# A chained gated MLP: one block split sooner, a sum's transfer put in front, the second gate before the first value

## The chip, the cores and the metric

The program runs on one core of a Trainium2 chip. A core has a matmul engine (PE in the profile, with its weight loads as PEld), a vector engine (DVE), an activation engine (ACT), a general engine (POOL) and a queue engine for loads (SP). Each runs its own list of instructions in order and waits on semaphores of the others. POOL issues the transfers that add while they copy; SP issues the plain loads. The metric is device time of one execution in microseconds.

## The reference

A trunk of two layers over 512 tokens of width 1024. Each layer has a token mixer, a cross attention into 256 memory tokens, and a gated MLP with a causal convolution of width 3 on its gate branch. The change lies in the MLP, and in the order of two loads for the attention's queries.

```python
def conv_ffn(x, norm, w_up, dw_w, dw_b, w_down):
    h = rms_norm(x, norm) @ w_up              # 1024 -> 2 * 3072
    g = causal_dwconv(h[..., :D_FF], dw_w, dw_b)
    u = h[..., D_FF:]
    return (jax.nn.gelu(g) * u) @ w_down      # 3072 -> 1024

for layer in range(DEPTH):                    # DEPTH = 2
    x = x + mixer(...)
    x = x + cross_attn(...)
    x = x + conv_ffn(...)
return rms_norm(x, final_norm)
```

## The kernel before

Data lies transposed, channels on the 128 partitions and the 512 tokens along the row. Every product is made of three matmuls of float32 operands that are split into a high part (ACT copies it, line 812) and a low part (DVE subtracts, line 819): high by high, high by low, low by high (lines 186 to 188).

The hidden width of 3072 is 24 chunks of 128. In each MLP the chunks 0 and 1 are computed plainly in `opening`; the chunks 2 to 23 are computed one by one in `unit(c)`, gate and value together, by a scheme with seven products instead of eight on blocks of half size. Its weight operands, by the names in the code, are `a11`, `a12`, `a22` (stored blocks) and `s1`, `s2`, `s3`, `s4` (sums of blocks). The sums are made in place by POOL's adding transfers (`low`, lines 817 to 830). A chunk's tile `raw` has two halves, `r` (first `a11`) and `z`:

- after the split of `a11`: `r += z` (line 822), and `r` is `s3`;
- after the split of `s3`: `r += a22` (line 826), and `r` is `s2`;
- after the split of `a22`: `z += a22` (line 824), and `z` is `s1`;
- after the split of `s2`: `r += a12` (line 830), and `r` is `s4`.

For the queries (tiles with a `ring`) both additions of `a22` stand at `s3` (lines 826 and 828).

Each of the seven products is twelve matmuls of 256 columns, called a piece here. PE's order in `unit(c)` is: `s1`, `s2`, `a12`, `s3`, then from unit 4 on 24 matmuls of the down projection, then `a11` of the next chunk (in `ahead`), `s4`, `a22`. `s2` adds onto a bank that ACT has filled from `a11`'s result (line 924), `s3` adds onto a bank that ACT has read first (line 941), and `s4` adds onto a bank that DVE has read first (line 171).

While PE works through unit c, ACT and DVE do two things between each other's steps, in the order of the code. They split blocks: in unit c the `s3`, `a22`, `a12`, `s1` and `s2` of chunk c+1, the `a11` of chunk c+2 and the `s4` of chunk c. And they finish the activation of chunk c-1 (`gating`: line 901 scale, 891 and 894 convolution, 896 GELU, 910 and 915). The order on PE, ACT, DVE and POOL is the order of the code in this part (`manual_schedule`); SP's order comes from the scheduler.

In `opening`, `start(i)` is the product of one plain weight piece, `gate(c)` is the scale, convolution and GELU of a plain chunk (lines 1012, 891, 894, 896, 1015), `values(c)` multiplies the value in and copies the high part (1018, 1020), `close(c)` makes the low part (1023). The token norm's mean is two matmuls (lines 287 and 288), followed by a root on ACT (1037) and a reciprocal on DVE (1040).

"First", "second" and "third unit" are chunks 2, 3 and 4. Units 2 and 3 have no down projection in them.

Of the kernel before, what the change touches and what calls it, by code (L numbers as in the profile page):

```python
# [61 lines left out]
def trunk(ctx: ExitStack, tc: tile.TileContext, I: dict, out: list):  # L62
    nc = tc.nc
    V, A, G, PE = nc.vector, nc.scalar, nc.gpsimd, nc.tensor
# [6 lines left out]
    tmp = ctx.enter_context(tc.tile_pool(name="tmp", bufs=8))  # L71
# [7 lines left out]
    def nm(s):  # L79
        uid[0] += 1  # L80
        return f"{s}_{uid[0]}"
# [16 lines left out]
    def main_ps():  # L98
        return psum.tile([P, T], F32, tag="mm", name=nm("mm"))
# [79 lines left out]
    def low(src, hi, lo=None):  # L179
        lo = act_r() if lo is None else lo  # L180
        V.tensor_tensor(lo, src, hi.bitcast(F32), op=ALU.subtract)  # L181
        return hi, lo
# [596 lines left out]
    class Blocks:  # L779
# [8 lines left out]
            self.r, self.z = raw[:, :T], raw[:, T:]  # L788

        def load_second(self):  # L790
            self.a22, self.a12 = [tmp.tile([P, T + 4], F32, tag="h", name=nm("wa"), bufs=4)[:, :T] for _ in range(2)]
            nc.sync.dma_start(self.a22, self.src[:, D : D + T])
            nc.sync.dma_start(self.a12, self.src[:, D + T :])

        def high(self, name):
            if self.ring:
# [20 lines left out]
        def low(self, name):  # L817
            hi, lo = self.w[name]
            V.tensor_tensor(lo, self.block(name), hi.bitcast(F32), op=ALU.subtract)  # L819

            if name == "a11":
                G.dma_start(self.r, self.z, accum_op=ALU.add)  # L822
            elif name == "a22" and not self.ring:
                G.dma_start(self.z, self.a22, accum_op=ALU.add)
            elif name == "s3":
                G.dma_start(self.r, self.a22, accum_op=ALU.add)  # L826
                if self.ring:
                    G.dma_start(self.z, self.a22, accum_op=ALU.add)
            elif name == "s2":
                G.dma_start(self.r, self.a12, accum_op=ALU.add)  # L830

# [3 lines left out]
    def ffn(layer, norm, nxt, seven, pairs):  # L835
# [37 lines left out]
        def high(c, name):  # L873
            if c in pairs and (c, name) not in done:
                pairs[c].high(name)

        def low(c, name):
            if c in pairs and (c, name) not in done:
                pairs[c].low(name)
                done.add((c, name))  # L880

        def times_r(out, ps, at):
            V.tensor_tensor(out[:, at], ps, norm.r[:, at], op=ALU.mult)
# [36 lines left out]
        def ahead(c):  # L920

            G, F = main_ps()[:, :M], main_ps()[:, :M]
            m(c, G, "a11", seven.B11)
            A.activation(F, G, AF.Copy)
            return G, F

        def unit(c):

            nonlocal left, chains
            G, F = chains  # L930
            down, seeded = downs.get(c), c > GC
            H = main_ps()[:, :M]
            m(c, H, "s1", seven.T1)
            high(c + 1, "s3")
            next(left, None)
            low(c + 1, "s3")

            m(c, F, "s2", seven.T2, False)
            next(left, None)
            u, f, g = tmp_f(), tmp_f(), tmp_f()  # L940
            A.activation(u[:, :M], F, AF.Copy)
            next(left, None)
            high(c + 1, "a22")

            m(c, G, "a12", seven.B21, False)
            next(left, None)
            if down:
                d = [down.bank(i, seeded) for i in range(2)]
            next(left, None)
            low(c + 1, "a22")  # L950
            times_r(g, G, left_half)
            high(c, "s4")

            m(c, F, "s3", seven.T3, False)
            A.activation(u[:, M:], F, AF.Copy)
            low(c, "s4")
            add(f[:, right_half], H, u[:, M:])
            V.tensor_tensor(f[:, right_half], f[:, right_half], norm.r[:, right_half], op=ALU.mult)
            high(c + 2, "a11")
            low(c + 2, "a11")  # L960
            high(c + 1, "a12")
            low(c + 1, "a12")
            if down:
                for ks in (range(GC - 1), (GC - 1,)):
                    for i in range(2):
                        down.products(i, d[i], seeded, ks)
            if c + 3 in pairs:
                pairs[c + 3].load()
            if c + 2 in pairs and c > first:
                pairs[c + 2].load_second()  # L970
            if c >= GC - 1 and c + 1 in downs:
                downs[c + 1].w.high()
                downs[c + 1].w.low()
            if c + 2 in downs and c + 2 <= CF:
                downs[c + 2].load()
            high(c + 1, "s1")
            low(c + 1, "s1")
# [12 lines left out]
            left = gating(c, g, f, u, F, H)  # L990
            next(left)

        def opening():
# [23 lines left out]
            def values(c):  # L1017
                V.tensor_tensor(y[c], ps.pop(2 * c + 1), y[c], op=ALU.mult)
                ys[c] = act_r(), act_r()
                A.activation(ys[c][0], y[c], AF.Copy)  # L1020

            def close(c):
                V.tensor_tensor(ys[c][1], y[c], ys[c][0].bitcast(F32), op=ALU.subtract)

            def both(c, name):
                high(c, name)
                low(c, name)

            ss = split(norm.ss)
            start(0)  # L1030
            fetch(2)
            w[-1].low()
            start(1, range(1))
            mean = mean_of(ss)
            Norm.due = None
            root = tmp_f()
# [1 line left out]
            A.activation(small.tile([P, 1], F32, tag="warm", name=nm("gelu"), bufs=1), eps, AF.Gelu_apprx_tanh)  # L1038
            norm.r = small.tile([P, T], F32, tag="r", name=nm("r"), bufs=1)
            V.reciprocal(norm.r, root)  # L1040
            start(1, range(1, C))
            pairs[second].load()
            pairs[second].load_second()
            fetch(3)
# [6 lines left out]
            t = seven.sums(3, lambda: (next(g), next(g)))  # L1051
# [2 lines left out]

            start(2)
            both(second, "a11")
            values(0)
            next(t, None)
            close(0)

            start(3)
            g = gate(1)
            next(g)
            both(second, "a22")
            next(g)
            next(g)
            next(g, None)
            chains = ahead(first)

            def rest():  # L1070
# [7 lines left out]
        first, second = PLAIN, PLAIN + 1  # L1078
# [807 lines left out]
```

## Time and profile before

| | |
|---|---|
| median of 3 runs | 1448.69 us (1446.52 to 1449.44) |
| profiled execution | 1447.83 us, of it 1446.0 us span |
| PE busy | 1424.8 us (99%) |
| DVE, ACT, POOL busy | 1079.0, 906.1, 318.2 us |
| mean granted PE clock | 0.997 |
| first MLP: opening to unit 4 | about 340 to 423 us from the span's start |
| second MLP: the same | about 1035 to 1119 us |

PE is busy nearly everywhere, so a change can only show where PE waits or runs at a lower clock. The two MLPs run the same code 695.41 us apart (first matmul of `ahead(first)`: 379.73 and 1075.14 us).

In a row of the timeline the columns are the start in us, the duration, engine, line, operation, output and inputs, count, and in brackets the engine's idle time before it with what ended it. Matmul durations overlap: a matmul of 256 columns is shown with 0.28 us, and the next starts 0.12 us after it. In a row of a stretch the columns are the stretch, its length, the busy time and count of each engine, the granted PE clock, the share of the DMA engines and GB/s.

### The profile page before, as it was taken

What the parts mean: (1) busy time and instruction counts of PE and PEld (TensorE: products, weight loads), DVE (VectorE), ACT (ScalarE), POOL (GpSimd) and SP (SyncE); (2) the same over time, 40 slices, a digit from 0 to 9 for tenths busy, and PEclk for the clock granted to TensorE, in tenths of its full rate; (3) what the DMA queues carried; (4) which work ended last, traced back from release to release, by engine and by line L of the source; (5) the groups of instructions that cost most, each with busy time, mean ns of one, the idle gap of its engine ahead of it and who ended that gap; (6) DMA issues with size and microseconds to landing.
All of it is one profiled execution on the core that took longest, in us unless ns stands there. A gap on an engine that the chain in (4) does not pass through costs nothing.

```text
span 1446.0 us, 22842 instructions
## 1 busy us (share of the span) xinstructions
PE 1424.8 (99%) x8650; PEld 1264.9 (87%) x8650; DVE 1079.0 (75%) x1796; ACT 906.1 (63%) x1592; POOL 318.2 (22%) x333
## 2 busy tenths in 40 slices
PE   9999999999999999999999999999998999999998
PEld 7888888988889999999988777898888999999997
DVE  6987776779776676676789997877787776676665
ACT  7678755667556666666655547667654665666664
POOL 0011310100122222222008992011002222222211
PEclk9999999999999999999999999999999999999999
DMA  8623232544487677677432364345437777777651
GB/s 294 199 77 99 88 131 68 119 112 140 103 188 177 161 175 175 156 181 166 131 126 88 117 176 144 96 96 131 114 99 178 171 181 163 164 181 165 162 130 59
DMA packets 80318, 205.36 MB, mean 142 GB/s; under 512 B 9040, under 2 KB 9552, under 8 KB 80208
## 3 DMA queue, kind: packets, MB, share of 16 engines
q1 hardware_dynamic: 51120, 151.20, 33.6%
q0 software_dynamic: 28800, 52.44, 20.7%
q8 instruction: 67, 1.10, 0.3%
q14 instruction: 43, 0.35, 0.1%
q10 hardware_dynamic: 288, 0.27, 0.1%
HBM read 146.21 MB, written 2.10 MB: 103 GB/s over the span
## 4 chain that ended last, share of the span: by engine, by line
PE 80%; issue 7%; DMA 5%; DVE 4%; ACT 2%; POOL 2%; SPq 0%; POOLq 0%; ACTq 0%; DVEq 0%
PE mm L188 19%; PE mm L187 19%; PE mm L186 19%; PE aux L186 7%; PE aux L187 7%; PE aux L188 7%; DMA raw<-wa 1%; PE mm L458 1%; DMA raw<-raw 1%; DMA raw<-in_wv 1%; DVE wlo L167 1%; POOL actf L1487 1%; ACT whi L166 1%; POOL act L167 0%; DMA wa<-in_wpair 0%
## 5 line engine op out<-in xcount | busy, mean ns | idle before, releaser
L186 PE MATMUL mm<-act,whi 128*128 128x512 f32 (+2 forms) x1061 | 369.4, 349 | 1.1 <-ACT whi L801 1.1
L187 PE MATMUL mm<-act,whi 128*128 128x512 f32 (+2 forms) x1061 | 369.4, 348 | 0.7 <-DVE act L181 0.4
L188 PE MATMUL mm<-act,wlo 128*128 128x512 f32 (+2 forms) x1061 | 369.1, 348 | 0.0
L186 PEld LDWEIGHTS mm<-act,whi 128*128 128x128 f32 x1061 | 200.6, 189 | 29.1 <-ACT whi L801 1.5
L187 PEld LDWEIGHTS mm<-act,whi 128*128 128x128 f32 x1061 | 200.8, 189 | 28.3 <-DVE act L167 1.0
L188 PEld LDWEIGHTS mm<-act,wlo 128*128 128x128 f32 x1061 | 200.8, 189 | 24.9 <-DVE wlo L167 0.6
L186 PE MATMUL mm<-bigr,bigr 128*128 128x256 f32 x704 | 201.3, 286 | 6.2 <-ACT bigr L812 4.0
L188 PE MATMUL mm<-bigr,bigr 128*128 128x256 f32 x704 | 200.8, 285 | 0.4 <-DVE bigr L819 0.4
L187 PE MATMUL mm<-bigr,bigr 128*128 128x256 f32 x704 | 200.5, 285 | 0.0
L812 ACT ACTIVATE bigr<-raw 128x512 fp32r<-128x512 f32 x176 | 105.2, 621 | 81.1 <-DMA raw<-wa 76.2
L186 PE MATMUL aux<-act,whi 128*128 128x512 f32 x399 | 155.8, 391 | 0.0
L187 PE MATMUL aux<-act,whi 128*128 128x512 f32 x399 | 155.7, 390 | 0.0
L188 PE MATMUL aux<-act,wlo 128*128 128x512 f32 x399 | 155.2, 389 | 0.0
L166 ACT ACTIVATE whi<-raw 128x1024 fp32r<-128x1024 f32 (+1 forms) x95 | 96.5, 1020 | 87.1 <-PE mm L187 46.4
L819 DVE TENSOR_TENSOR bigr<-raw,bigr 128x512 fp32r<-128x512 f32 x176 | 117.7, 688 | 41.9 <-ACT bigr L812 41.9
L186 PEld LDWEIGHTS mm<-bigr,bigr 128*128 128x128 f32 x704 | 136.4, 194 | 7.5 <-ACT bigr L812 4.4
L188 PEld LDWEIGHTS mm<-bigr,bigr 128*128 128x128 f32 x704 | 136.5, 194 | 0.9 <-DVE bigr L819 0.9
L187 PEld LDWEIGHTS mm<-bigr,bigr 128*128 128x128 f32 x704 | 136.5, 194 | 0.0
L822 POOL DMA_DIRECT2D raw<-raw x50 | 43.3, 866 | 361.4 <-DVE wlo L819 223.9
L171 DVE TENSOR_TENSOR tmp<-mm,tmp 128x256 f32<-128x256 f32 x130 | 53.9, 419 | 86.3 <-PE mm L188 84.6
L167 DVE TENSOR_TENSOR wlo<-raw,whi 128x1024 fp32r<-128x1024 f32 (+1 forms) x75 | 90.3, 1210 | 22.0 <-ACT whi L166 21.7
L826 POOL DMA_DIRECT2D raw<-wa x50 | 43.2, 863 | 282.2 <-DVE bigr L819 229.4
(355 smaller groups left out, 3122.4 us busy)
## 6 DMA issues: line engine op xcount, KB each, us to landing
raw<-wa POOLq DMA_DIRECT2D x150, 256.0 KB, 5.2
wa<-in_wpair SPq DMA_DIRECT2D x88, 256.0 KB, 3.4
raw<-in_wpair SPq DMA_DIRECT2D x44, 512.0 KB, 4.8
big<-in_wdown SPq DMA_DIRECT2D x44, 512.0 KB, 4.0
raw<-raw POOLq DMA_DIRECT2D x50, 256.0 KB, 4.5
raw<-in_pw SPq DMA_DIRECT2D x24, 512.0 KB, 3.3
raw<-in_win SPq DMA_DIRECT2D x20, 512.0 KB, 3.3
raw<-in_wk SPq DMA_DIRECT2D x16, 512.0 KB, 3.6
```

What stands on the lines that cost most here:

```text
L166: A.activation(hi, src, AF.Copy)
L167: fetched[1] = (eng or V).tensor_tensor(lo, src, hi.bitcast(F32), op=ALU.subtract)
L171: V.tensor_tensor(out, a, b, op=ALU.add)
L186: PE.matmul(ps, wh, xh, start=first, stop=False, skip_group_check=onto)
L187: PE.matmul(ps, wh, xl, start=False, stop=False, skip_group_check=onto)
L188: PE.matmul(ps, wl, xh, start=False, stop=last, skip_group_check=onto)
L458: PE.matmul(p, m[j], x, start=k == 0 and j == 0 and x is hi, stop=k == C - 1 and x is lo)
L812: A.activation(self.w[name][0], self.block(name), AF.Copy)
L819: V.tensor_tensor(lo, self.block(name), hi.bitcast(F32), op=ALU.subtract)
L822: G.dma_start(self.r, self.z, accum_op=ALU.add)
L826: G.dma_start(self.r, self.a22, accum_op=ALU.add)
L1487: G.tensor_tensor(z[:, s:], z[:, s:], f[:, s:], op=ALU.add)
```

## The change

Five edits, all in the order of instructions; no arithmetic is added or taken away.

1. In `unit`, in the first unit alone: the split of `a11` of chunk 4 (and with it the issue of `r += z` of chunk 4) moves from the unit's fourth step to its first.
2. In `low`, for the MLP's chunks: `z += a22` moves from the split of `a22` to the split of `s3`, and stands there in front of `r += a22`.
3. In `opening`: `gate(1)` begins before `values(0)`; the low parts of the sums, `close(0)` and the end of `gate(1)` follow later.
4. In `opening`: the mean's two matmuls stand behind six matmuls of the second plain product instead of three.
5. In `load_second`: the queries' `a12` is loaded before `a22`; for the MLP's chunks the order stays.

```diff
         def load_second(self):
-            self.a22, self.a12 = [tmp.tile([P, T + 4], F32, tag="h", name=nm("wa"), bufs=4)[:, :T] for _ in range(2)]
-            nc.sync.dma_start(self.a22, self.src[:, D : D + T])
-            nc.sync.dma_start(self.a12, self.src[:, D + T :])
+            for name in ("a12", "a22") if self.ring else ("a22", "a12"):
+                block = tmp.tile([P, T + 4], F32, tag="h", name=nm("wa"), bufs=4)[:, :T]
+                setattr(self, name, block)
+                at = D + T if name == "a12" else D
+                nc.sync.dma_start(block, self.src[:, at : at + T])
...
             if name == "a11":
                 G.dma_start(self.r, self.z, accum_op=ALU.add)
-            elif name == "a22" and not self.ring:
-                G.dma_start(self.z, self.a22, accum_op=ALU.add)
             elif name == "s3":
-                G.dma_start(self.r, self.a22, accum_op=ALU.add)
-                if self.ring:
-                    G.dma_start(self.z, self.a22, accum_op=ALU.add)
+                for block in (self.r, self.z) if self.ring else (self.z, self.r):
+                    G.dma_start(block, self.a22, accum_op=ALU.add)
...
             next(left, None)
             low(c + 1, "s3")
+            if c == first:
+                both(c + 2, "a11")
...
-            high(c + 2, "a11")
-            low(c + 2, "a11")
+            both(c + 2, "a11")
...
-            start(1, range(1))
+            start(1, range(2))
             mean = mean_of(ss)
...
-            start(1, range(1, C))
+            start(1, range(2, C))
...
             start(2)
             both(second, "a11")
-            values(0)
-            next(t, None)
-            close(0)
-
-            start(3)
             g = gate(1)
             next(g)
+            values(0)
             both(second, "a22")
             next(g)
             next(g)
+            next(t, None)
+            close(0)
             next(g, None)
+
+            start(3)
             chains = ahead(first)
```

A block that is already split is passed over by the later call (`done`). Line numbers shift a little: 812, 819, 891, 924 and 941 become 814, 821, 894, 927 and 946; the adding transfers of lines 822, 826/824 and 830 become 824, 827 and 829.

The order on ACT at the end of the opening and in the first unit, before (812 is the high part of a block, 1020 the high part of a finished chunk):

```order
L812 ACTIVATE whi_3698<-raw_3631 128x512
L1020 ACTIVATE act_3704<-tmp_3644 128x512
L891 ACTIVATE tmp_3739<-tmp_3737,par 128x512
L812 ACTIVATE bigr_3741<-wa_3633 128x512
L896 ACTIVATE tmp_3739<-tmp_3739 128x512
L924 ACTIVATE mm_3750<-mm_3749 128x256
L812 ACTIVATE bigr_3777<-raw_3631 128x512
L1020 ACTIVATE act_3780<-tmp_3739 128x512
L941 ACTIVATE tmp_3798<-mm_3750 128x256
L812 ACTIVATE bigr_3815<-raw_3040 128x512
L955 ACTIVATE tmp_3798<-mm_3750 128x256
L812 ACTIVATE whi_3833<-raw_3647 128x512
```

The last row here, the high part of chunk 4's `a11`, stands behind everything else of the first unit's first four steps. With the change the same place reads:

```order
L814 ACTIVATE whi_3698<-raw_3631 128x512
L894 ACTIVATE tmp_3705<-tmp_3703,par 128x512
L1024 ACTIVATE act_3708<-tmp_3644 128x512
L814 ACTIVATE bigr_3711<-wa_3633 128x512
L899 ACTIVATE tmp_3705<-tmp_3705 128x512
L927 ACTIVATE mm_3749<-mm_3748 128x256
L814 ACTIVATE bigr_3776<-raw_3631 128x512
L1024 ACTIVATE act_3779<-tmp_3705 128x512
L814 ACTIVATE whi_3785<-raw_3647 128x512
L946 ACTIVATE tmp_3803<-mm_3749 128x256
```

The first convolution step of gate 1 (891, now 894) moved ahead of the finished value, and the high part of chunk 4's `a11` (`raw_3647`) moved ahead of two bank reads and one block.

The order of POOL's transfers for the chunks 3 (`raw_709_3631`), 4 (`raw_717_3647`) and 5 (`raw_746_3840`), before:

```order
L822 DMA raw_709_3631<-raw_709_3631 128x512
L824 DMA raw_709_3631<-wa_710_3633 128x512
L826 DMA raw_709_3631<-wa_710_3633 128x512
L822 DMA raw_717_3647<-raw_717_3647 128x512
L830 DMA raw_709_3631<-wa_711_3634 128x512
L826 DMA raw_717_3647<-wa_718_3649 128x512
L824 DMA raw_717_3647<-wa_718_3649 128x512
L822 DMA raw_746_3840<-raw_746_3840 128x512
```

Chunk 3's `z += a22` (824) stands alone behind `r += z`, and chunk 4's pair has `r` (826) in front. With the change, where "x2" at line 827 is `z += a22` and then `r += a22`:

```order
L824 DMA raw_709_3631<-raw_709_3631 128x512
L827 DMA raw_709_3631<-wa_710_3633 128x512 x2
L824 DMA raw_717_3647<-raw_717_3647 128x512
L829 DMA raw_709_3631<-wa_711_3635 128x512
L827 DMA raw_717_3647<-wa_718_3649 128x512 x2
L824 DMA raw_746_3840<-raw_746_3840 128x512
```

POOL's sequence of chunks is the same; within each pair `z` now goes first, and for chunk 3 `z += a22` no longer goes out alone behind `r += z` but together with `r += a22`.

More of the change, by code (lines that the diff above doesn't have):

```diff
@@ L880, in low, with both @@
                 done.add((c, name))
+        def both(c, name):
+            high(c, name)
+            low(c, name)
         def times_r(out, ps, at):
@@ L1023, in close @@
                 V.tensor_tensor(ys[c][1], y[c], ys[c][0].bitcast(F32), op=ALU.subtract)
-            def both(c, name):
-                high(c, name)
-                low(c, name)
             ss = split(norm.ss)
```

## The prediction

> **What bounds the kernel now.** I read the page first, then PE's waits, then stretches around them, then the chain of waits.
>
> ```profile
> PE 1424.8 (99%) x8650; PEld 1264.9 (87%) x8650; DVE 1079.0 (75%) x1796; ACT 906.1 (63%) x1592; POOL 318.2 (22%) x333
> ```
>
> PE is the bound, and the change removes no matmul, so all it can win is lost PE time. PE's waits in the first MLP from `ahead(first)` to unit 4, and around the same place of the second:
>
> ```profile
> PE mm L186 <- ACT bigr L812: 1.9, 1, 1.9
> PE mm L186 <- DVE tmp L171: 0.7, 1, 0.7
> PE mm L186 <- ACT mm L924: 0.6, 1, 0.6
> PE mm L186 <- ACT tmp L941: 0.4, 1, 0.4
> PE mm L188 <- DVE bigr L819: 0.2, 1, 0.2
> ...
> PE mm L186 <- ACT bigr L812: 2.0, 1, 2.0
> PE mm L186 <- ACT tmp L941: 0.8, 1, 0.8
> PE mm L186 <- DVE tmp L171: 0.7, 1, 0.7
> ...
> PE stat L288 <- DVE act L167: 0.2, 1, 0.2
> ```
>
> What these stretches really lose is more than the waits. Two rows of PE, 72 matmuls apart without a wait, give (394.94 - 386.30)/6 = 1.44 us for a piece of twelve:
>
> ```profile
> 386.30 0.28 PE L186 MATMUL mm<-bigr,bigr 128*128 128x256 f32 x1
> 394.94 0.28 PE L186 MATMUL mm<-act,whi 128*128 128x256 f32 x1
> ```
>
> From `ahead(first)` to the start of unit 4's `s3` piece there are 18 pieces, 25.9 us. The first two rows below are that span in the two MLPs: 32.45 and 32.89 us, so 6.5 and 7.0 us are lost.
>
> ```profile
> 379.73:412.18 32.45, 28.68 (x218) 27.66 (x216) 23.46 (x40) 16.83 (x33) 7.66 (x10) 0.95 0.68 155
> 1075.14:1108.03 32.89, 28.68 (x217) 27.66 (x216) 23.46 (x40) 16.80 (x33) 7.66 (x10) 0.95 0.66 153
> 403.57:405.79 2.22, 0.28 (x4) 0.08 (x2) 0.02 (x1) 0.69 (x2) 0.00 (x0) 1.00 0.94 171
> 405.79:410.74 4.95, 4.73 (x25) 4.52 (x25) 4.33 (x8) 2.44 (x5) 0.86 (x1) 0.66 0.83 214
> 872.64:877.00 4.36, 4.36 (x23) 2.92 (x24) 1.90 (x4) 2.04 (x3) 3.06 (x2) 1.00 0.58 203
> ```
>
> The third and fourth rows show the second part of the loss: after the long wait the granted clock is 0.66 for 4.95 us, which costs 4.95 x 0.34 = 1.7 us. Waits 3.8, clock 1.7, and about 1.0 for slow restarts behind five waits make the 6.5. The chain of waits names the cause of the long one:
>
> ```profile
> 390.14 5.21 DMA raw<-raw
> ...
> 395.45 0.64 ACT bigr L812
> ...
> 396.11 0.70 DVE bigr L819
> ...
> 397.10 0.46 POOL raw L826
> ...
> 397.64 7.44 DMA raw<-wa
> ...
> 405.11 0.64 ACT bigr L812
> ```
>
> Chunk 4's `r += z` goes out at 390.14; only then `s3` is split, and only then `r += a22` and `z += a22` start; `s1` waits for the second of them until 405.08. Everything on ACT and DVE behind that late `s3` (the bank reads 941 and 171) is late too.
>
> **The opening (edit 3).** DVE's and ACT's rows in the first MLP:
>
> ```profile
> 374.89 0.69 DVE L819 TENSOR_TENSOR wlo<-raw,whi 128x512 fp32r<-128x512 f32 x1 [0.56 <-ACT whi L812]
> 378.05 0.68 DVE L1012 TENSOR_TENSOR tmp<-mm,r 128x512 f32<-128x512 f32 x1
> 380.74 1.53 DVE L894 SCALAR_TENSOR_TENSOR tmp<-tmp,par,tmp 128x511 f32<-128x511 f32 x2
> 384.44 0.68 DVE L819 TENSOR_TENSOR bigr<-raw,bigr 128x512 fp32r<-128x512 f32 x1
> 382.37 0.63 ACT L896 ACTIVATE tmp<-tmp 128x512 f32<-128x512 f32 x1 [2.27 <-DVE tmp L894]
> 382.90 0.37 ACT L924 ACTIVATE mm<-mm 128x256 f32<-128x256 f32 x1
> ```
>
> Gate 1's scale (1012) moves up to 375.7, right behind `a11`'s low part; its product is done, since the next one, 24 matmuls of 512 columns at about twice 0.12, ends at 379.73. Then come the value product (0.6), 1.3 of waiting for ACT to finish the convolution's first step, the finished value and `a22`'s high part, then `a22`'s low part (0.6): the convolution starts at 378.9 instead of 380.74, GELU ends at 381.2 instead of 383.0, and the bank copy 924 starts when its piece is done, 381.3, well ahead of the `s2` piece at 379.73 + 2 x 1.44 = 382.6. So the 0.6 us wait and its restart go. What is put off, four low parts of the sums (1.3) and `close(0)`, is done by 382.3; the sums' first low part is needed at 382.4 and done at 380.8. The low part of chunk 3's `s3` ends at 384.2 (380.4 + 1.3 + three of 0.6 + 0.7) instead of 385.1. If that cover were gone, the price is the old wait, 0.8.
>
> **The mean (edit 4)** stands three matmuls later, about 0.7 us in the first MLP, where PE did not wait; reciprocal and gate 0 follow, but 0.5 of it vanishes in DVE's wait for a weight piece, and 0.2 is left, which is in the times above. In the second MLP the three matmuls fill the wait at line 288: PE wins about 0.6 in front of the stretch, and the mean is not later. I take 0 for the sum, since the gate behind it is what sets the end (below); bounds -0.2 to +0.6. **The queries (edit 5)** read no block that PE waits for: the two loads swap, and the SP order and the tile releases stay. 0.
>
> **Chunk 3 (edit 2).** `z += a22` now starts with `r += a22` at 384.5, and `r` 0.54 behind it at 385.05. Before, `r` went alone, and SP had just begun a load:
>
> ```profile
> 382.79 0.33 SPq L195 DMA_DIRECT2D big<-in_wdown  x1
> ```
>
> ```profile
> 385.41 0.86 POOL L826 DMA_DIRECT2D raw<-wa  x1 [5.09 <-DVE bigr L819]
> ```
>
> Prices of transfers, first of a pair and second of a pair in the query stage, where few loads run, then the second and the first of a pair in the units 3 to 6, beside two loads of SP:
>
> ```profile
> DMA to landing us min/median/max: 3.3/3.4/3.4
> ...
> DMA to landing us min/median/max: 4.3/4.3/4.3
> ...
> DMA to landing us min/median/max: 6.7/7.3/8.2
> ...
> DMA to landing us min/median/max: 3.6/6.1/6.6
> ```
>
> By 385 most of that load is over and SP's next one waits for this very pair, so I take the query stage, and up to 0.6 more for `z`: `z` lands at 387.9 to 388.6, `r` at T = 389.4 to 389.9. `s1` and `s2` of chunk 3 are needed at 379.73 + 8 x 1.44 = 391.3 and 392.7 and are split by 390 and 391.2: hidden, with 1.5 us of cover.
>
> **Chunk 4 (edits 1 and 2).** Its `a11` is split at 385.5, three matmul pieces of ACT and DVE work that have room in the first unit (941 still ends 0.4 ahead of the `s3` piece), so `r += z` goes out behind chunk 3's pair and lands near 391, where it was 395.35. `s3` no longer waits for it; it waits for its place in the queue, behind gate 2's work, which starts after chunk 3's `s2`:
>
> ```profile
> 390.36 1.28 DVE L819 TENSOR_TENSOR bigr<-raw,bigr 128x512 fp32r<-128x512 f32 x2
> 393.32 1.54 DVE L894 SCALAR_TENSOR_TENSOR tmp<-tmp,par,tmp 128x511 f32<-128x511 f32 x2 [0.55 <-ACT tmp L891]
> 405.77 1.29 DVE L819 TENSOR_TENSOR bigr<-raw,bigr 128x512 fp32r<-128x512 f32 x2 [2.30 <-ACT bigr L812]
> 410.94 0.38 ACT L941 ACTIVATE tmp<-mm 128x256 f32<-128x256 f32 x1
> ```
>
> From T: high part 0.7, low part 0.7, then as in these rows 393.32 - 391.64 = 1.7 to the convolution, 1.5 of it, `s3`'s low part 0.6, POOL's issue 0.3: chunk 4's pair starts at T + 5.5 = 395.1, two microseconds before 397.10. Its second transfer before took 0.54 + 7.44 = 8.0 from the pair's start; the longest row gives 0.5 + 8.2 = 8.7. So `r` lands 403.1 to 404.1 against 405.08 for the last transfer before. `z`, in front, lands between 398.8 and 401.7 (3.6 to 6.6 in the last row above). `s1`'s piece is due at 379.73 + 15 x 1.44 = 401.3, and 0.4 later because DVE's bank read 171 ends at T + 9.2: **the long wait goes**, 0.7 at most is left. What is late next is gate 3's chain: `s2` split, bank read 941, then unit 4's `s3` piece. Before, it ran from 407.06 (low part done) to 411.32; that is 4.3. From `r`'s landing it is 0.7 + 0.7 + 4.3 = 5.7. So unit 4's `s3` piece starts at 408.8 to 409.8, middle 409.2, against 412.18: **3.0 us won** in the first MLP, of 6.5 lost. In the second the chain runs 0.2 earlier and the old start was 0.4 later (1108.03 - 695.41 = 412.62): **3.6 us**. After that piece 24 matmuls of the down projection give the chain room; PE showed no wait in the later units, and there the swap lets the last split follow the last landing by one copy instead of two. I take 0 for them.
>
> Sum: 6.6. On the profiled execution 1447.83 - 6.6 = 1441.2; the median of the runs lies 0.9 above it, so **1442.1 us**.
>
> The clock: of the 3.5 us still lost before unit 4's `s3` piece about 0.5 falls at `s4` of unit 3, 0.5 at `s1` and 1 at `s2` of unit 4 (its high part is ready 0.7 after `r` lands, and the bank copy 0.3 later), and 1.5 at `s3`, with 1.4 to 2.9 of matmuls between them. The longest comparable wait that left the clock at 1.00 ended at 872.64 (the last row of the stretches):
>
> ```profile
> PE stat L298 <- DVE actf L1502: 1.7, 1, 1.7
> ```
>
> So I expect no slow stretch. [...]
>
> **Rivals.**
> - *The clock still falls.* Two of the new waits may fall close together. Each slow stretch gives 1.7 back: 1443.8 with one, 1445.5 with two, and up to 1448.6 if `r` is late as well (405.1, as the second transfer was: 1.5 more in each MLP). For it: the old slow stretch came after 0.7 and 1.9 and 0.2 close together. Against: 872.64. 20%.
> - *The slow stretch comes whatever the wait.* If PE slows 4 us after the units without a down projection for a reason that stays, 3.4 of the sum stay lost: 1445.5. For it: both MLPs show it at the same place. Against: it begins within a microsecond of the longest wait both times. 5%. [...]
> - *The transfers land early.* If the pair lands as in the query stage, DVE's queue alone is left: `s1`'s low part behind a weight piece (line 203) at 402.2, `s2` behind it, so `s3` at 407.1: 5.1 and 5.7, sum 10.8, 1437.9. Against: two loads of SP start within a microsecond of the pair. 10%.
> - *Slower.* Chunk 3's `r += a22` now stands second, with chunk 4's `r += z` right behind it. If the three share the engines as the pairs of the later units do, it lands 8.2 after its issue, at 393.3; `s2` of chunk 3 is then 1.3 late, and by the same chain (T + 19.5) unit 4's `s3` starts at 412.8: slower by 0.6 in the first MLP, even in the second, and two more slow stretches would cost 3.4: 1449.3 to 1452.7. It decides from T = 412.2 - 19.5 = 392.7 on. Against: no load of SP runs then. 5%.
> - *The early split does nothing*, because the queue and not the transfer held `s3`: excluded by ACT's wait for `raw<-raw` until 395.35.
>
> **How the numbers follow.** Forecast 60%, clock 20%, staying slow stretch 5%, early 10%, slower 5%. A measurement of this kernel tells about 0.2% (2.9 us) from no change. Faster by more: all of forecast and early, half of the two clock cases: 0.82. Same: their other half and a part of slower: 0.14. Slower: 0.04. The range goes from the early case, 1437.9, to 1446.8, between two slow stretches and these with a late `r`.
>
> **What would show it.** Right: no wait at 924; ACT's `s3` of chunk 4 without a wait for `raw<-raw`; the pair's start near 395; PE's long wait for line 814 gone and a wait for 946 in unit 4 of 1 to 2 us in its place; clock 1.00 through both stretches; the two stretches 29.4 and 29.3 us. Wrong: chunk 3's `r += a22` landing after 391, a clock below 1, or waits in the later units.

## The result: 0.66% faster

The changed kernel takes 1437.81 us (median), the kernel before 1448.41 in the same session: a ratio of 0.9934, 95% interval 0.9914 to 0.9953. One of its five runs took 3739.67 us, for a reason that nothing here shows, and is left out of the ratio. The medians differ by 10.6 us, the means that the ratio compares by 9.6. Forecast were 1442.1 us and a range from 1437.9 to 1446.8, so the sign was right and the gain larger than the 6.6 us forecast. The median lies at the fast end of the range, 0.1 us outside it as it stands; the ratio, on the 1448.69 that the forecast started from, gives 1439.1. Timed a second time, beside other kernels, the ratio was 0.9932 (0.9915 to 0.9949).

The profiled execution of the change took 1440.97 us, the longest of the four that the ratio counts, with a span of 1439.2 us for 1446.0 before. Its busy time, and PE's waits in the first and in the second MLP around the place of the change:

```profile
PE 1421.0 (99%) x8650; PEld 1263.3 (88%) x8650; DVE 1079.1 (75%) x1796; ACT 910.2 (63%) x1592; POOL 317.4 (22%) x333
...
PE mm L186 <- ACT tmp L946: 1.2, 1, 1.2
...
PE mm L186 <- ACT tmp L946: 3.9, 2, 3.7
PE mm L186 <- DVE tmp L171: 0.4, 1, 0.4
```

The 1.9 and 2.0 us for `s1`'s high part (line 812 of before) are gone in both MLPs, and so is the wait at the bank copy 924. In their place stands a wait for ACT's copy of the `s2` result (946 in the change, 941 before), 1.2 us in the first MLP and 3.7 in the second. The same stretches as before the change, from `ahead(first)` to unit 4's `s3` piece, and the five microseconds behind the second:

```profile
378.89:406.45 27.56, 26.38 (x218) 25.97 (x216) 23.54 (x43) 15.71 (x31) 7.89 (x10) 1.00 0.81 184
1068.82:1099.93 31.11, 26.83 (x217) 26.01 (x215) 23.88 (x44) 15.75 (x31) 7.81 (x9) 1.00 0.71 162
1099.93:1104.90 4.97, 4.97 (x21) 4.40 (x22) 4.24 (x9) 4.07 (x8) 0.86 (x1) 0.66 0.95 193
```

The first stretch went from 32.45 to 27.56, the second from 32.89 to 31.11: 4.9 and 1.8 won. The clock is 1.00 in both, but 0.66 behind the wait of 3.7. The rest of the difference in span is small: 0.8 ahead of the first stretch (379.73 to 378.89; the two traces part by 1.3 in the first 100 us, in code that is the same, so this is not the change's), 0.6 between the two stretches (before 1075.14 - 412.18 = 662.96, now 1068.82 - 406.45 = 662.37), and 1.3 given back behind the second. 4.9 + 1.8 + 0.8 + 0.6 - 1.3 = 6.8.

Where the first MLP's gain comes from is seen on POOL, before and then after (the adding transfers; column one is the issue):

```profile
375.89 0.86 POOL L822 DMA_DIRECT2D raw<-raw  x1 [27.34 <-DVE wlo L819]
379.46 0.86 POOL L824 DMA_DIRECT2D raw<-wa  x1 [2.71 <-DMA raw<-raw]
385.41 0.86 POOL L826 DMA_DIRECT2D raw<-wa  x1 [5.09 <-DVE bigr L819]
390.14 0.86 POOL L822 DMA_DIRECT2D raw<-raw  x1 [3.87 <-DVE wlo L819]
...
397.10 0.86 POOL L826 DMA_DIRECT2D raw<-wa  x1 [4.30 <-DVE bigr L819]
397.64 1.21 POOL L824 DMA_DIRECT2D raw<-wa  x1
```

```profile
375.24 0.86 POOL L824 DMA_DIRECT2D raw<-raw  x1 [27.54 <-DVE wlo L821]
378.81 0.86 POOL L827 DMA_DIRECT2D raw<-wa  x1 [2.71 <-DMA raw<-raw]
383.84 0.86 POOL L827 DMA_DIRECT2D raw<-wa  x1 [4.17 <-DVE bigr L821]
385.16 0.86 POOL L824 DMA_DIRECT2D raw<-raw  x1 [0.46 <-DMA big<-in_wdown]
389.69 0.86 POOL L829 DMA_DIRECT2D raw<-wa  x1 [3.66 <-DVE bigr L821]
390.23 1.22 POOL L827 DMA_DIRECT2D raw<-wa  x1
393.50 0.86 POOL L827 DMA_DIRECT2D raw<-wa  x1 [2.06 <-DVE bigr L821]
```

Chunk 3's three transfers leave as before: `z += a22` alone, released by the landing of `r += z` (2.71 <- DMA raw<-raw), and `r += a22` five microseconds later, by itself too. What has moved is chunk 4: `r += z` from 390.14 to 385.16, `z += a22` from 397.64 (behind `r`) to 390.23 (3.3 ahead of `r`), `r += a22` from 397.10 to 393.50. The prediction, and the sentence in the description of the change that `z` now goes out together with `r`, are wrong here: the place of `z` in the program is at `s3`'s split, but it stands in front of `r` on POOL and reads nothing that the split writes, so of chunk 4's own steps it waits for `r += z` alone. In chunk 3 it leaves at that landing. In chunk 4 the landing is at 385.16 + 3.8 = 388.96, and `z` leaves at 390.23, right behind chunk 3's `r += a12` (line 829, 389.69), which stands ahead of it on POOL.

### The profile page after: what moved, and what is told of

It reads as the page before. It is cut to its first block, busy times and chain, and to the rows that moved or that the text cites. A ratio compares the mean times of both kernels' runs of the same rounds, so it can differ in the third digit from the quotient of the medians.

```text
span 1439.2 us, 22840 instructions
## 1 busy us (share of the span) xinstructions
PE 1421.0 (99%) x8650; PEld 1263.3 (88%) x8650; DVE 1079.1 (75%) x1796; ACT 910.2 (63%) x1592; POOL 317.4 (22%) x333
## 4 chain that ended last, share of the span: by engine, by line
PE 82%; issue 6%; DMA 4%; DVE 3%; POOL 2%; ACT 2%; SPq 0%; POOLq 0%; DVEq 0%; ACTq 0%
PE mm L187 19%; PE mm L186 19%; PE mm L188 19%; PE aux L186 7%; PE aux L187 7%; PE aux L188 7%; PE mm L458 2%; DMA raw<-wa 1%; DMA raw<-raw 1%; DMA raw<-in_wv 1%; DMA wa<-in_wpair 1%; DVE wlo L167 1%; POOL actf L1487 1%; POOL act L167 1%; PE aux L532 1%
## 5 line engine op out<-in xcount | busy, mean ns | idle before, releaser
L827 POOL DMA_DIRECT2D raw<-wa x100 | 88.4, 904 | 283.9 <-DVE bigr L821 151.1
L814 ACT ACTIVATE bigr<-raw 128x512 fp32r<-128x512 f32 x176 | 109.5, 624 | 55.1 <-DVE wlo L203 38.5
L821 DVE TENSOR_TENSOR bigr<-raw,bigr 128x512 fp32r<-128x512 f32 x176 | 121.0, 688 | 12.9 <-ACT bigr L814 9.5
```

Of the source, the lines that this page charges most:

```text
L814: A.activation(self.w[name][0], self.block(name), AF.Copy)
L827: G.dma_start(block, self.a22, accum_op=ALU.add)
```

## The experiments

The theory that these rows suggest, called "leaves alone" below: `z += a22`, set in front, goes out as soon as `r += z` has landed and POOL has sent what stands ahead of it, and so is out of the way when `r` goes; this matters for chunk 4, and it and the early block each bring a part. The rivals are named with each run. The stretches in this table are those from `ahead(first)` to unit 4's `s3` piece in the profiled executions; one without any loss would be 25.9.

| kernel | ratio to before (95%) | first stretch, us | second, us |
|---|---|---|---|
| before | 1 | 32.45 | 32.89 |
| the change | 0.9934 (0.9914 to 0.9953) | 27.56 | 31.11 |
| the change, again | 0.9932 (0.9915 to 0.9949) | 26.88 | 28.82 |
| edit 2 alone | 0.9967 (0.9955 to 0.9979) | 30.28 | 31.49 |
| edit 1 alone | 0.9972 (0.9962 to 0.9983) | 30.62 | 31.28 |
| edits 3 and 4 alone | 0.9988 (0.9980 to 0.9997) | 31.33 | 33.78 |
| change without edit 2 | 0.9958 (0.9946 to 0.9971) | 29.55 | 31.46 |
| change, z held in all chunks | 0.9981 (0.9972 to 0.9989) | 31.15 | 33.82 |
| change, z held in chunk 3 | 0.9954 (0.9942 to 0.9966) | 29.56 | 30.51 |
| change, z held in chunk 4 | 0.9956 (0.9944 to 0.9968) | 29.06 | 30.14 |
| change, one load less | 0.9947 (0.9934 to 0.9959) | 27.41 | 29.39 |
| change, copy first in all units | 1.0045 (1.0033 to 1.0057) | 27.28 | 28.49 |
| change, copy first in unit 4 | 0.9912 (0.9899 to 0.9926) | 26.24 | 27.35 |
| the last and one load less | 0.9935 (0.9921 to 0.9948) | 26.24 | 27.01 |

### Edit 2 alone

```diff
-            elif name == "a22" and not self.ring:
-                G.dma_start(self.z, self.a22, accum_op=ALU.add)
             elif name == "s3":
-                G.dma_start(self.r, self.a22, accum_op=ALU.add)
...
+                for block in (self.r, self.z) if self.ring else (self.z, self.r):
+                    G.dma_start(block, self.a22, accum_op=ALU.add)
```

> The kernel before with edit 2 alone (z += a22 in front of r += a22, nothing else). Theory 'leaves alone' (z += a22 depends only on the landing of r += z, so it goes out ahead of s3's split and r follows by itself): chunk 3's transfers stay as they were (379.5 and 385.4), since z went out at the landing of r += z there already. Chunk 4's z goes out at 395.6, right behind the landing of r += z at 395.35, and no longer at 397.64; r stays at 397.1 and lands near 404. The wait at s1 of unit 4 falls from 1.9 to under 1, unit 4's s3 piece starts near 409.8 (r's landing + 5.7) and not 412.2: about 2.4 per MLP, 1443 to 1445. Rival 'the early block does it all' (edit 1 alone removes the wait, the order of the two transfers is worth nothing): within 1 us of the kernel before, 1447.5 to 1449.

Measured: 1441.5 us beside 1446.44 before, so 4.9 us. POOL's rows of chunk 4, and the two stretches:

```profile
388.69 0.86 POOL L822 DMA_DIRECT2D raw<-raw  x1 [3.88 <-DVE wlo L819]
...
394.57 0.86 POOL L825 DMA_DIRECT2D raw<-wa  x1 [3.21 <-DMA raw<-raw]
396.04 0.86 POOL L825 DMA_DIRECT2D raw<-wa  x1 [0.61 <-DVE bigr L819]
```

```profile
378.57:408.85 30.28, 27.24 (x217) 26.12 (x215) 23.06 (x40) 15.68 (x32) 7.35 (x10) 1.00 0.74 169
1071.00:1102.49 31.49, 28.07 (x217) 27.46 (x215) 23.06 (x40) 16.13 (x32) 7.61 (x10) 0.95 0.72 162
```

`z` goes at 394.57, right behind the landing of `r += z`, as the theory says, although `r += z` is as late as before (10.1 behind the stretch's start, before 10.4). The wait for `s1` is gone, and the order of two transfers on one queue is worth half of the whole change by itself. The gain is the 2.4 in each MLP that was expected (by the medians; the two stretches show 3.6 of the 4.9). The expected 1443 to 1445 was missed because the kernel before was 2 us faster here than in the first measurement; the same holds for the next two runs. The rival that the early block does it all falls.

### Edit 1 alone

```diff
             low(c + 1, "s3")
+            if c == first:
+                high(c + 2, "a11")
+                low(c + 2, "a11")
```

> The kernel before with edit 1 alone (chunk 4's a11 split in unit 3's predecessor, the first unit; order of transfers, opening, mean and queries as before). Theory 'leaves alone': r += z of chunk 4 goes out near 386 and lands near 390, s3 is split by 395, r += a22 goes out near 395 and z += a22 0.5 behind it; s1 waits for z, the second to land, near 402.5 to 403.5: a wait of 1 to 2 us at s1 stays, unit 4's s3 starts near 410: 2 per MLP, 1443 to 1445.5. Rival 'the early block does it all': the wait is gone and it stands within 1.5 us of the whole change, 1437 to 1440.

Measured: 1442.53 us, 3.9 less than before. PE's waits in the first and the second MLP, and the stretches:

```profile
PE mm L186 <- ACT bigr L812: 2.1, 1, 2.1
...
PE mm L186 <- ACT bigr L812: 2.2, 1, 2.2
```

```profile
379.19:409.81 30.62, 28.12 (x217) 27.42 (x216) 23.47 (x40) 16.34 (x33) 7.14 (x10) 0.94 0.72 164
1071.64:1102.92 31.28, 28.30 (x218) 27.47 (x216) 23.47 (x40) 16.48 (x33) 7.24 (x10) 0.95 0.66 161
```

The wait for `s1` stays as long as it was, since `z` still leaves behind `r`, and the clock still falls behind it, to 0.53 and 0.50 in the three microseconds from the end of the wait. What is won is that all of it happens earlier against the waits that came later (941 is no longer among them).

### The opening and the mean alone

This kernel is the change without edits 1, 2 and 5: of its diff, the part in `opening` alone.

> The kernel before with edits 3 and 4 alone (second gate ahead of the first value; the mean three matmuls later). Both theories: the wait at the bank copy (line 924 of before) goes, 0.8 per MLP, and the second MLP's wait for the mean, 0.6; chunk 4's transfers go out at most 0.7 earlier, so the long wait at s1 shrinks by no more than that: 1445.5 to 1447.5. A third reading, that the opening alone moves r += z of chunk 4 far enough for the long wait to go, would give under 1443.

Measured: 1444.66 us, 1.8 less.

```profile
378.54:409.87 31.33, 28.35 (x218) 27.54 (x216) 23.93 (x43) 16.48 (x32) 7.75 (x10) 0.95 0.70 160
1071.17:1104.95 33.78, 29.65 (x218) 29.05 (x217) 24.19 (x44) 16.57 (x32) 7.94 (x10) 0.90 0.67 149
```

1.1 is won in the first stretch and 0.9 lost in the second, where the clock is lower still (0.90 for 0.95 before); it holds a new wait for the copy of the `s2` result (945 in this kernel):

```profile
PE mm L186 <- ACT tmp L945: 2.6, 1, 2.6
```

Between the stretches lie 1071.17 - 409.87 = 661.30 us, before 662.96, while the two kernels without edit 4 above have 662.15 and 661.83. In the ten profiles with edit 4 (without the one whose units are all longer, below) it is 660.6 to 662.4, in the three without 661.8 to 663.0. So the mean's new place may be worth about 1 us there, which is not shown: no run has it by itself, and the two ranges overlap.

Edit 5 has no run by itself either. The first stretch begins at 378.54 to 379.73 in the four kernels without it and at 378.33 to 379.98 in those with it, so nothing of it shows; a few tenths of a microsecond could hide there.

The three parts alone sum to 3.3 + 2.8 + 1.2 = 7.3 thousandths, and the whole is 6.6 to 6.8. They add within their intervals.

### The change without edit 2

```diff
-            elif name == "s3":
-                for block in (self.r, self.z) if self.ring else (self.z, self.r):
-                    G.dma_start(block, self.a22, accum_op=ALU.add)
+            elif name == "a22" and not self.ring:
+                G.dma_start(self.z, self.a22, accum_op=ALU.add)
+            elif name == "s3":
+                G.dma_start(self.r, self.a22, accum_op=ALU.add)
...
```

> The whole change without edit 2: z += a22 again goes out at a22's split, behind r += a22; the early block, the opening, the mean and the queries as in the change. Theory 'z's early departure is worth as much beside the early block as alone': r += z of chunk 4 lands early, r += a22 goes out near 393.5 and z 0.5 behind it, both landing 400 to 402; s1 of unit 4 waits 1 to 2 us for z, and the granted clock falls behind it where the wait is near 1.9: 0.33% slower than the whole change by what edit 2 gave alone, 1440.5 to 1442.5 on a kernel before of 1447. Rival 'with the early block and the opening together the second transfer is in time anyway': within 1 us of the whole change, no wait at s1.

Measured: 1439.72 us on a kernel before of 1446.14, 0.9958. Its waits in the two MLPs:

```profile
PE mm L186 <- ACT bigr L814: 1.4, 1, 1.4
...
PE mm L186 <- ACT bigr L814: 2.3, 1, 2.3
```

The wait for `s1` is back, and edit 2 is worth about 2.5 thousandths (3.6 us) beside the others; the intervals of this kernel and of the change still overlap a little. The rival that the second transfer would be in time anyway falls.

### z held until s3 is split

This is what the prediction took the change to be.

```diff
             elif name == "s3":
+                if not self.ring:
+                    held = small.tile([P, 1], F32, tag="held", name=nm("held"), bufs=1)
+                    G.tensor_copy(held, lo[:, T - 1 : T].bitcast(F32))
                 for block in (self.r, self.z) if self.ring else (self.z, self.r):
```

> The whole change, but POOL copies one column of s3's low part ahead of z += a22, so that z cannot leave before s3 is split and the two transfers go out as a pair, as the prediction had it. Theory 'leaves alone': z goes out at 383.8 in chunk 3 and r 0.5 behind it, r lands 388 to 389 and not 387.2; in chunk 4 the pair goes out together near 394 and r lands 402 to 403.5 and not 400.7; unit 4's s3 starts 1.5 to 2.5 later than with the whole change, so 1440.5 to 1443, near the predicted 1442.1. Rival 'transfers land early in any case' (the pair is as fast as two single ones): within 1 us of the whole change, 1437 to 1438.8.

Measured: 1443.67 us, 0.9981 of before, where the change, in the next session, had 0.9932: 7 us of its gain are gone, more than expected. POOL's rows, then the landing times of the second and third transfer from the view of the transfers (KB, us), and the stretches:

```profile
383.12 0.18 POOL L828 COPY held<-bigr 128x1 f32<-128x1 f32 x1 [7.59 <-DVE bigr L821]
383.63 1.75 POOL L830 DMA_DIRECT2D raw<-wa  x2 [0.33 <-issue]
384.72 1.55 POOL L824 DMA_DIRECT2D raw<-raw  x1
```

```profile
raw<-wa POOLq DMA_DIRECT2D x1, 256.0 KB, 6.5
...
raw<-raw POOLq DMA_DIRECT2D x1, 256.0 KB, 8.6
```

```profile
378.33:409.48 31.15, 27.56 (x218) 26.18 (x216) 23.73 (x43) 16.01 (x31) 7.51 (x11) 1.00 0.70 160
1071.03:1104.85 33.82, 27.82 (x217) 26.24 (x215) 24.02 (x44) 15.92 (x31) 7.54 (x11) 1.00 0.65 148
```

Chunk 3's pair and chunk 4's `r += z` are on the way at once, with a load of SP that now begins at 385.87. `r += a22` lands at 390.65 (6.5 behind its issue at 384.17) and `r += z` 8.6 behind its own. In the change each of these had 3.3 and 3.8:

```profile
raw<-wa POOLq DMA_DIRECT2D x1, 256.0 KB, 3.3
...
raw<-raw POOLq DMA_DIRECT2D x1, 256.0 KB, 3.8
```

So the prediction's forecast for its own picture was too low as well: 409.2 - 379.73 = 29.5 for a stretch that takes 31.15.

### z held in chunk 3 alone, and in chunk 4 alone

The same edit for one chunk of each MLP. The change itself ran beside them.

```diff
+                if getattr(self, "hold", False):
...
+        pairs[PLAIN + 1].hold = True
```

(`PLAIN + 2` in the second of them.)

> The whole change once more, beside the three kernels below on the same chip. Both theories: 0.9914 to 0.9953 of the kernel before. If the wait ahead of unit 4's s3 piece in the second MLP (3.7 us in the profiled run, behind a late r += z of chunk 5) is a matter of two transfers that meet by chance, its length differs in this run's trace; if it belongs to the code, it is 3 to 4 us again.

> The whole change with z += a22 held until s3 is split in chunk 3 only. If what the prediction got wrong in chunk 3 (z and r leave as a pair) is what matters, because then three transfers (z, r, and r += z of chunk 4) run at once: r += z of chunk 4 takes over 8 us as in the kernel with all held, s3 of chunk 4 is split 2 to 3 us later, and most of the loss of that kernel is here: 1441 to 1444. If it is chunk 4's pair that matters: within 1 us of the whole change.

> The whole change with z += a22 held until s3 is split in chunk 4 only. Chunk 3's transfers as in the whole change; chunk 4's pair leaves together near 393.5, z lands 397 to 400 and r 401.5 to 402.5 (7.2 for the first, 8.0 to 8.7 for the second of a pair): unit 4's s3 piece 1 to 1.5 later per MLP, 1439.5 to 1441.5. If chunk 3's hold does it all: within 1 us of the whole change.

Measured: 1436.64 us for the change, 1440.37 with chunk 3 held, 1440.23 with chunk 4 held. By the medians each costs 3.6 to 3.7 us, and the two together 7 (0.9981 against 0.9932), so both chunks matter, and in the change both have `z` out of the way. The interval of each alone overlaps that of the change; that of both together does not. The 1440.23 lies in the range that was expected if chunk 4 matters, but the other half of each text, that one of the two chunks carries the loss, was wrong: chunk 3 costs as much and no more.

The change's second trace also answers what the 3.7 us wait is. Its stretches, and its wait for the copy in the second MLP:

```profile
379.95:406.83 26.88, 26.37 (x218) 25.96 (x216) 23.42 (x43) 15.82 (x31) 7.86 (x10) 1.00 0.82 187
1068.33:1097.15 28.82, 26.82 (x218) 26.01 (x216) 23.83 (x44) 15.70 (x31) 7.81 (x9) 1.00 0.74 175
```

```profile
PE mm L186 <- ACT tmp L946: 1.4, 2, 1.3
```

It is 1.3 here. In the first trace the copy 946 stood on ACT behind chunk 5's `s3`, and that behind a transfer of 8.5 us (issue 1089.84) that two loads of SP had joined; ACT's rows:

```profile
1098.46 0.63 ACT L814 ACTIVATE bigr<-raw 128x512 fp32r<-128x512 f32 x1 [4.33 <-DMA raw<-raw]
...
1099.52 0.36 ACT L946 ACTIVATE tmp<-mm 128x256 f32<-128x256 f32 x1
```

In the second trace the same transfer took 6.1 us; the two loads began 0.3 and 0.7 us ahead of it there, and 0.1 and 0.5 behind it in the first. So the second stretch (31.11 and 28.82 us) and the clock in the five microseconds behind it (0.66 and 1.00) vary from one execution to the next. That the order of these three transfers makes the difference is an estimate from these two traces and was not tried.

### The copy ahead of the late work

If the wait left is a copy in a queue, putting it in front should remove it. First in all units (`s3`'s split goes behind the copy from the second unit on):

```diff
-            high(c + 1, "s3")
+            if c == first:
+                high(c + 1, "s3")
             next(left, None)
...
             m(c, F, "s2", seven.T2, False)
-            next(left, None)
             u, f, g = tmp_f(), tmp_f(), tmp_f()
             A.activation(u[:, :M], F, AF.Copy)
             next(left, None)
+            if c > first:
+                high(c + 1, "s3")
+            next(left, None)
...
```

> The whole change with ACT's copy of the s2 result (line 946 of the change) set ahead of the GELU, and s3's split of the next chunk behind both from unit 3 on. If the wait that is left ahead of unit 4's s3 piece (1.2 in the first MLP, 3.7 in the second) is a copy that stands on ACT behind chunk 5's late r += z and behind the GELU, it goes in both: 1.2 and up to 3.7 plus 1.3 of clock in the profiled run, 1 to 4 us faster than the whole change on the medians. If that wait is only the next limit of many (s1 or s2 of chunk 5 then come late, since s3 of chunk 5 is split later): within 1 us of the whole change, with the wait one unit later.

Measured: 1453.99 us, 17 more than the change. The wait for the copy is gone from the stretch, but each of the units 5 to 22 now waits once for the bank copy (line 854) that stands behind `s3` and the GELU on ACT. All such waits, and two of them, one unit apart:

```profile
PE aux L186 <- ACT aux L854: 6.0, 36, 0.2
```

```profile
455.38 0.50 PE L186 MATMUL aux<-act,whi 128*128 128x512 f32 x1 [0.17 <-ACT aux L854]
...
471.38 0.50 PE L186 MATMUL aux<-act,whi 128*128 128x512 f32 x1 [0.17 <-ACT aux L854]
```

From one to the next it is 15.99 us; the same two matmuls of the change lie at 454.99 and 470.52, 15.54 apart. With its wait of 0.17 us and what follows on it a unit thus takes 0.45 us more, and 36 x 0.45 = 16 of the 17 us.

The rival's "next limit" holds, in a place that the expectation did not name and at a price far outside both of its ranges. The next kernel has the new order in unit 4 alone; another takes out a load of 512 KB that the first unit repeats (the edit below); the last does both.

```diff
-            if c + 2 in downs and c + 2 <= CF:
+            if c + 2 in downs and c + 2 <= CF and c > first:
                 downs[c + 2].load()
```

> The whole change with the copy of the s2 result ahead of the GELU and of s3's split in unit 4 alone, all other units as in the change. If the 17 us that the same order cost in all units were the bank copies of the later units (36 waits at line 854) and nothing in unit 4, these are gone and the wait ahead of unit 4's s3 piece is under 0.5 in both MLPs: 1 to 2.5 faster than the whole change on the medians (1434.5 to 1436 on a kernel before of 1447). If unit 4 only passes the wait on to unit 5: within 0.7 of the whole change.

> The whole change without the second of two loads of the first down-projection piece (the first unit loads again, at 382 in the first MLP, 512 KB that the opening has loaded already; the computation is the same). If that load is what makes chunk 3's r += a22 take 5.0 in the second MLP where it takes 3.3 in the first, r lands 1 to 1.7 earlier there, and unit 4's s3 piece with it: 1 to 1.7 faster than the whole change. If it is mostly over by then and the transfers slow each other: no change within 0.7.

> Both of the last two together. If both are gains, they add: 2 to 4 faster than the whole change (1433 to 1435 on a kernel before of 1447); if the piece that the opening loads is kept and its buffer held longer, something in the opening could wait for that buffer instead, and it is no faster than the one with the copy alone.

Measured: 1433.86, 1439.08 and 1436.22 us, on a kernel before of 1446.14. With the copy first in unit 4 the stretches, and the wait for the copy (949 in this kernel) in the second MLP, are:

```profile
378.36:404.60 26.24, 26.21 (x217) 26.01 (x216) 22.62 (x41) 14.75 (x29) 7.67 (x9) 1.00 0.81 187
1065.94:1093.29 27.35, 26.74 (x218) 26.12 (x216) 22.82 (x42) 14.94 (x29) 6.93 (x8) 1.00 0.75 174
```

```profile
PE mm L186 <- ACT tmp L949: 1.6, 1, 1.6
```

The first stretch is within 0.4 of one without loss. In the second 1.5 is won against the better trace of the change, and the 1.6 us wait stands in unit 5 instead: there the wait was passed on, as the rival said. Whether this kernel beats the change stays open: its ratio is 0.9912 (0.9899 to 0.9926) against 0.9932 (0.9915 to 0.9949), the intervals overlap, and the kernel with one load less on top, which has the same stretches, comes to 0.9935. It beats the kernel before clearly. The repeated load costs nothing that shows: without it chunk 3's `r += a22` takes 5.2 us in the second MLP, in the change 4.8 and 5.0, and the theory that it was the cause falls.

## Why the prediction came out, step by step

**What bounds the kernel** was right: PE is 99% busy before and after, and the gain is lost PE time in the two stretches.

**The opening** was right in its step: the wait at 924 is gone, and chunk 3's `r += a22` is issued 4.95 behind `ahead(first)` for 5.68 before. Alone, edits 3 and 4 bring 1.2 thousandths.

**The mean** was taken as 0, with +0.6 as the upper bound. The time between the stretches is 662.37 and 661.50 in the two traces of the change for 662.96 before: 0.6 and 1.5. If that is the mean's, which no run shows, the upper bound would have been the better value, and the cover that was claimed (the gate behind it sets the end) does not hold for the second MLP, where PE itself had waited.

**Chunk 3: the step that failed.** "`z += a22` now starts with `r += a22` at 384.5" is wrong. Counted from `ahead(first)`, its first two transfers stand within 0.2 us of where they stood, and `r += a22` is earlier by the opening's 0.7 alone. The row that shows it was in the profile of before: 379.46, released by the landing of `r += z` and not by a split. The forecast for `r`, T = 9.7 to 10.2 behind `ahead(first)`, came out as 383.84 + 3.3 - 378.89 = 8.3 in the first MLP. The price of the pair, had it been one, was wrong in the other direction: 390.65 - 378.33 = 12.3, with `z` held.

**Chunk 4** carried both errors on. `r += z` was forecast 11.3 behind the start and landed at 385.16 + 3.8 - 378.89 = 10.1. The pair's start was forecast at 15.4; `z` left at 390.23 - 378.89 = 11.3 and `r` at 14.6. `r` landed at about 21.8 (ACT's next split starts at 400.82, the moment it is in), where the forecast was 23.4 to 24.4:

```profile
400.82 0.63 ACT L814 ACTIVATE bigr<-raw 128x512 fp32r<-128x512 f32 x1 [1.56 <-DMA raw<-wa]
```

From there the chain to unit 4's `s3` piece takes 406.45 - 400.7 = 5.7, as forecast. So the first MLP won 4.9 and 5.6 in the two traces and not 3.0: the term was mis-sized by the landing of `r`, and its mechanism, the late `r` and the chain behind it, was right. In the second MLP 3.6 were forecast and 1.8 and 4.1 won; the low one is a wait for 946 of 3.7 where 1 to 2 was forecast. In the first trace 4.9 + 1.8 = 6.7 is nearly the forecast 6.6, and that is luck: the first MLP won 1.9 more than forecast and the second 1.8 less.

**The rival that transfers land early** gave 27.4 for the first stretch (407.1 - 379.73), and 27.56 and 26.88 were measured. It was the right number for the first MLP, by luck: it was to come from a pair that lands as in the query stage, the second in 4.3, and `r` took 400.7 - 393.5 = 7.2. It was given 10% because two loads of SP start within a microsecond of the pair. They do, and `r` is as slow as that argument had it; but it leaves earlier, and `z`, for which `s1` waits, is on its way 3.3 us before it.

**The rival of a slow stretch that comes whatever the wait** is excluded: with no wait over 1.3 us the clock is 1.00 through both stretches (the change's second trace), and with the wait back it falls again (0.94 and 0.95 over the stretches, in the change without edit 2 and with edit 1 alone). **The clock that still falls** came in the first trace alone, behind the 3.7 us wait. The prediction argued against it from the length of the waits; by the last section the length alone does not decide, so the 1.00 was in part luck: behind a wait of 1.8 us in the kernel with edit 2 alone (ending at 1089.53) the clock was 0.68 over three microseconds, behind one of 2.1 in the change with one load less (ending at 1096.64) 1.00. **The slower case** needed three transfers together, with 8.2 us for `r += a22`. The kernel that holds `z` has them. In the first MLP that one takes 6.5 and the `r += z` behind it 8.6, and the stretch stays 1.3 us shorter than before; in the second they take 8.6 and 9.2, and the stretch is 0.9 longer.

## What to carry to other kernels

In the change `z += a22` of chunk 3 stands in the program at `s3`'s split, and it left at 378.81, when `r += z` had landed, as it did at 379.46 before. So when a transfer leaves is read from what released it in the trace, and before a step is moved in the text it is worth a look whether that releaser moves with it. An adding transfer of 256 KB had no one price here: chunk 3's `r += a22` took 3.3 us in the first MLP of the change, 4.8 and 5.0 in the second, and 6.5 and 8.6 as the second of three; so its price is read from a row with the same company. And the copy that an engine makes for a waiting matmul should not stand behind work that waits for a transfer: PE waited 3.7 us for 946 behind chunk 5's `s3`. But with the copy ahead in all units the kernel took 17 us more than the change; with the copy ahead in unit 4 alone the second stretch fell from 28.82 to 27.35 us.

## What the runs showed of the hardware that was not expected

How long a wait of PE was did not alone decide in these runs whether the granted clock was lower behind it. Over fourteen profiles, of PE's waits of 0.95 us or more from 340 us on, one of the 17 below 1.35 us was followed by a granted clock under 1.00 in the next three microseconds, and of the 16 from 1.35 to 3.67 ten were.

In the kernel before, the clock was at 0.50 from 407.07 to 410.48 and from 1103.39 to 1106.80, beginning 1.3 and 1.75 us behind the ends of the waits of 1.9 and 2.0 us; in the first trace of the change it was at 0.50 from 1100.51 to 1103.92, beginning 0.6 behind the wait of 3.7. Each time that is 3.41 us at half, so 1.7 us. The rows below have this length too. The first two are the change without edit 2 around its wait of 1.4 us (ending at 402.94), the last two the kernel with `z` held in all chunks around the longest wait behind which the clock stayed at 1.00 (2.5 us, ending at 1086.86):

```profile
400.76:404.17 3.41, 1.83 (x13) 1.42 (x13) 1.68 (x4) 1.42 (x3) 0.00 (x0) 1.00 0.88 163
404.17:407.58 3.41, 3.41 (x18) 3.41 (x18) 2.79 (x7) 1.39 (x3) 0.86 (x1) 0.50 0.96 267
```

```profile
PE mm L186 <- ACT mm L930: 2.5, 1, 2.5
...
1082.65:1086.06 3.41, 1.74 (x15) 1.54 (x13) 0.16 (x1) 0.15 (x1) 0.00 (x0) 1.00 0.51 110
1086.06:1089.47 3.41, 2.61 (x20) 2.46 (x21) 2.31 (x5) 2.09 (x4) 0.88 (x1) 1.00 0.48 107
```

PE is busy for 1.83 us of the first row and the clock is 0.50 in the next; it is busy for 1.74 us of the third and the clock is 1.00 in the next. What makes the difference is not shown: no run was made to test it.
